# The MLP's first product by Strassen's seven block products, with the tokens stationary

## The chip, the cores and the metric

One Trainium2 chip, one NeuronCore of it. The metric is the device time of one execution in microseconds (us), as a median over runs. The engines named below are TensorE (matmuls, in the profile PE, its weight loads PEld), VectorE (DVE), ScalarE (ACT), GpSimd (POOL) and SyncE (SP, whose queue issues the loads).

## What is computed

A decoder trunk of two layers on 256 tokens of width 2048, all in float32. Each layer has a mixer (differential attention or dilated attention), attention into 256 memory tokens, an output projection, and an MLP with hidden width 8192. The part that matters here:

```
for i in range(DEPTH):                      # 2 layers
    h = _rmsnorm(x, g_attn[i])
    proj = h @ w_in[i]                      # queries, keys, values, memory queries
    ...
    x = x + merged @ w_out[i]
    hm = _rmsnorm(x, g_mlp[i])              # 256 x 2048
    x = x + jnp.square(jax.nn.relu(hm @ w_mlp1[i])) @ w_mlp2[i]   # 2048 x 8192, then 8192 x 2048
return _rmsnorm(x, g_final)
```

## The kernel before

**Precision.** Every large product is made of three. An operand is split into a high part, which TensorE's fp32r format holds, and the low rest; hi x hi, hi x lo and lo x hi are added. `split` does it: ScalarE copies the high part (line 108), VectorE subtracts it for the low part (line 109). Activations are split once; weights are split as they arrive, 1024 columns at a time (`weights`, into the tags whi and wlo with four buffers each), from loads of 1 MB (`load_weights`, tag raw, three buffers, issued by SP, line 72).

**The first product** (`mlp_up`) computes one chunk of 1024 hidden features in four blocks of 256 with `gemm_feat`. The weights are stationary there and the tokens move: for each of 16 row tiles and two halves of the block one matmul takes the high weights against high and low activations side by side (512 columns, line 142) and one the low weights against the high activations (256 columns, line 139). The result has features on the partitions and tokens along the columns. `feat_sum` adds its two halves (lines 214 and 216), VectorE squares its positive part (line 540), and a split writes the two parts of hT.

**The second product** (`mlp_down`) takes hT as the stationary operand and moves split weights of 512 columns (`gemm_tok_piece`, lines 161 to 163): 192 matmuls for a chunk, in four column blocks of 512 whose results go into PSUM tiles psd; two VectorE operations a block (line 562) add them to x.

**Order.** The program emits up(0), up(1), down(0), up(2), down(1), ..., up(7), down(6), down(7) for each layer. A scheduler then fixes the order on each engine before the kernel runs, and assigns buffers from the pools: an instruction whose buffer isn't free is placed where the buffer will be, and waits there on a semaphore. PSUM has two tiles of two banks (pool pmm, tag mm) and four of one bank (pool pat, tag at).

**Names.** ps_u, hi_u, lo_u, raw_u: first product; psd, hi_d, lo_d, raw_d: second product; pso, psv, ps_q, ps_k: output, value, query and key projections; xTm: the activations of the first product; lo_o and lo_d: low halves of weights; x_sb: the tokens.

Of the kernel before, what the change touches and what calls it, by code (L numbers as in the profile page):

```python
# [9 lines left out]
F32 = mybir.dt.float32  # L10
F32R = mybir.dt.float32r
# [6 lines left out]
P = 128  # L18
# [14 lines left out]
TMP = 6  # L33
GROUPS = ((128, 1), (512, 4), (2048, 16))
# [17 lines left out]
def trunk(ctx: ExitStack, tc: tile.TileContext, x, mem, g_attn, w_in, w_out, lambda_qk,  # L52
# [6 lines left out]
    apool = ctx.enter_context(tc.tile_pool(name="apool", bufs=8))  # L59
# [33 lines left out]
    # matmuls on zeros that bring the tensor engine to its full clock while the first loads run  # L93
    zero = const.tile([P, 512], BF16, name="zero")
# [16 lines left out]
    def weights(src, k, c, nm, raw=None):  # L111
        """k row tiles of c columns, k * c = 2048, as two (hi, lo) pairs of k/2 row tiles."""
        if raw is None:
            *_, raw = load_weights(src, k, c, nm)
        res = []
        for h in range(2):
            hi = wpool.tile([P, 1024], F32R, tag="whi", bufs=4, name=f"hi_{nm}_{h}")
            lo = wpool.tile([P, 1024], F32R, tag="wlo", bufs=4, name=f"lo_{nm}_{h}")
            split(hi, lo, raw[:, h * 1024:(h + 1) * 1024])
            for kk in range(k // 2):  # L120
                res.append((hi[:, kk * c:(kk + 1) * c], lo[:, kk * c:(kk + 1) * c]))
        return res

    def gemm_feat(w, acts, nm, raws=(None, None)):
        """[256 features, 256 tokens] as [128, 2, 2, 256]: the two halves of dim 2 add up."""
        ps = pmm.tile([P, 2, 512], F32, tag="mm", name=f"ps_{nm}")
        k0 = 0
        for pc in range(2):
            wt = weights(w[pc * 1024:(pc + 1) * 1024, :], 8, 256, f"{nm}_{pc}", raws[pc])
            for kk in range(8):  # L130
                k = k0 + kk
# [36 lines left out]
    def to_feat(src_of_tok, c, dst, gcol, nm):  # L168
        """tokens x 512 features (chunk c) -> features x tokens times g, split into dst."""
# [14 lines left out]

    def sumsq(src, acc):
# [8 lines left out]
    def rstd_of(ssq, nm):  # L194
        """ssq [128, 2, 4] -> 1 / rms by token [128, 2]."""
# [6 lines left out]
    def bcast_row(r, nm):  # L202
        """[128, 2] by token -> [128, 256], the tokens along the free axis in every partition."""
# [7 lines left out]
    def feat_sum(ps, nm):  # L211
        """the two halves of a gemm_feat result added: [128, 2, 256] in SBUF."""
# [437 lines left out]
```

## Time and profile before

| | us |
|---|---|
| median of 3 runs (2239.68 to 2239.79) | 2239.72 |
| span of the profiled execution | 2237.8 |
| TensorE busy in it | 2226.3 (99%) |
| VectorE busy | 1335.5 (60%) |
| ScalarE busy | 1040.7 (47%) |

The span runs from the first to the last instruction of one profiled execution. The median is 1.9 us above it. Busy time is the time in which an engine had an instruction under way, so neighbours that overlap are counted once there, while the mean duration of a group is that of one instruction by itself. The granted clock tells at which share of its full rate TensorE was allowed to run.

### The profile page before, as it was taken

The page shows a single profiled execution, that of the slowest core. Times are in us where ns is not written, and L with a number is a line of the kernel's source. Part 1 is how long each engine was busy: PE and PEld are TensorE (multiplying, and loading weights), DVE is VectorE, ACT ScalarE, POOL GpSimd, SP SyncE. Part 2 cuts the span into 40 slices and gives each one's busy share as a digit, 9 for nine tenths or more (in the row PEclk, how much of TensorE's full clock was granted, in tenths as well). Part 3 has the DMA queues.
Part 4 walks back from the last instruction along what each step waited for, and adds up shares of the span by engine and source line. Part 5 has one row for each costly group of instructions (what it writes and reads, how often), then busy time and mean ns, then how long its engine had stood idle before and what let it go on. Part 6 is the DMA issues. An engine that isn't in the chain of part 4 may idle for free.

```text
span 2237.8 us, 27970 instructions
## 1 busy us (share of the span) xinstructions
PE 2226.3 (99%) x11462; PEld 1885.6 (84%) x11462; DVE 1335.5 (60%) x1568; ACT 1040.7 (47%) x1362; POOL 14.0 (1%) x26
## 2 busy tenths in 40 slices
PE   9999999999999999999999999999999999999998
PEld 7888878888888888888888888888888888888887
DVE  7557765565555555555666665555656555555555
ACT  7445554544344444444455544454444444434443
POOL 0000000000000000000000000000000000000000
PEclk9999999999999999999999999999999999999999
DMA  8554454566656656666555455456665665665664
GB/s 266 189 178 161 151 169 162 177 187 188 190 188 188 193 186 192 192 189 193 191 187 166 156 170 188 151 188 188 188 189 188 188 188 190 187 195 188 188 203 148
DMA packets 304849, 411.96 MB, mean 184 GB/s; under 512 B 6529, under 2 KB 203346, under 8 KB 304722
## 3 DMA queue, kind: packets, MB, share of 16 engines
q1 hardware_dynamic: 304448, 410.02, 57.7%
q8 instruction: 89, 1.46, 0.3%
q14 instruction: 38, 0.31, 0.0%
q10 hardware_dynamic: 274, 0.17, 0.0%
HBM read 408.07 MB, written 2.10 MB: 183 GB/s over the span
## 4 chain that ended last, share of the span: by engine, by line
PE 98%; DMA 1%; ACT 0%; issue 0%; DVE 0%; SPq 0%; POOL 0%; POOLq 0%; DVEq 0%
PE ps_u L142 21%; PE ps_u L139 11%; PE psd L163 10%; PE psd L162 10%; PE psd L161 10%; PE ps_q L142 4%; PE ps_k L142 4%; PE pso L163 3%; PE pso L161 3%; PE pso L162 3%; PE ps_q L139 2%; PE ps_k L139 2%; PE psv L163 2%; PE psv L162 2%; PE psv L161 2%; PE ps_km L142 1%
## 5 line engine op out<-in xcount | busy, mean ns | idle before, releaser
L142 PE MATMUL ps_u<-xTm,hi_u 128*128 128x512 f32 x2048 | 720.3, 398 | 0.0
L139 PE MATMUL ps_u<-xTm,lo_u 128*128 128x256 f32 x2048 | 564.9, 281 | 0.0
L142 PEld LDWEIGHTS ps_u<-xTm,hi_u 128*128 128x128 f32 x2048 | 381.5, 188 | 89.3
L109 DVE TENSOR_TENSOR lo_u<-raw_u,hi_u 128x1024 fp32r<-128x1024 f32 x256 | 313.1, 1224 | 232.3 <-ACT hi_u L108 230.4
L109 DVE TENSOR_TENSOR lo_d<-raw_d,hi_d 128x1024 fp32r<-128x1024 f32 x252 | 308.3, 1223 | 235.7 <-ACT hi_d L108 233.5
L108 ACT ACTIVATE hi_d<-raw_d 128x1024 fp32r<-128x1024 f32 x252 | 267.3, 1061 | 347.7 <-PE psd L163 293.2
L108 ACT ACTIVATE hi_u<-raw_u 128x1024 fp32r<-128x1024 f32 x256 | 271.1, 1059 | 286.9 <-PE ps_u L142 188.8
L163 PE MATMUL psd<-hi_d,hT 128*128 128x512 f32 x1008 | 392.6, 389 | 0.0
L161 PE MATMUL psd<-hi_d,hT 128*128 128x512 f32 x1008 | 392.4, 389 | 0.0
L162 PE MATMUL psd<-lo_d,hT 128*128 128x512 f32 x1008 | 392.3, 389 | 0.0
L139 PEld LDWEIGHTS ps_u<-xTm,lo_u 128*128 128x128 f32 x2048 | 386.7, 189 | 5.9
L162 PEld LDWEIGHTS psd<-lo_d,hT 128*128 128x128 f32 x1008 | 189.2, 188 | 39.4
L163 PEld LDWEIGHTS psd<-hi_d,hT 128*128 128x128 f32 x1008 | 189.2, 188 | 39.3
L161 PEld LDWEIGHTS psd<-hi_d,hT 128*128 128x128 f32 x1008 | 189.2, 188 | 38.8
L142 PE MATMUL ps_q<-xT,hi_q 128*128 128x512 f32 x384 | 138.0, 399 | 0.0
L142 PE MATMUL ps_k<-xT,hi_k 128*128 128x512 f32 x384 | 136.7, 395 | 0.0
L139 PE MATMUL ps_k<-xT,lo_k 128*128 128x256 f32 x384 | 108.2, 287 | 0.0
L139 PE MATMUL ps_q<-xT,lo_q 128*128 128x256 f32 x384 | 107.9, 286 | 0.0
L562 DVE SCALAR_TENSOR_TENSOR x_sb<-psd,rsq,x_sb 128x512 f32<-128x512 f32 x126 | 88.8, 746 | 24.4 <-PE psd L163 24.4
L214 ACT ACTIVATE fb_u<-ps_u 128x512 f32<-128x512 f32 x64 | 38.3, 598 | 119.0 <-PE ps_u L142 119.0
L216 DVE TENSOR_TENSOR ft_u<-ps_u,fb_u 128x512 f32<-128x512 f32 x64 | 44.3, 692 | 78.8 <-ACT fb_u L214 78.8
L109 DVE TENSOR_TENSOR lo_v<-raw_v,hi_v 128x1024 fp32r<-128x1024 f32 x48 | 58.8, 1225 | 49.7 <-ACT hi_v L108 49.6
(272 smaller groups left out, 2767.2 us busy)
## 6 DMA issues: line engine op xcount, KB each, us to landing
raw_u<-in_w_mlp_dram SPq DMA_DIRECT2D x128, 1024.0 KB, 5.7
raw_d<-in_w_mlp_dram SPq DMA_DIRECT2D x126, 1024.0 KB, 5.1
raw_q<-in_w_in_dram SPq DMA_DIRECT2D x24, 1024.0 KB, 5.2
raw_k<-in_w_in_dram SPq DMA_DIRECT2D x24, 1024.0 KB, 5.1
raw_v<-in_w_in_dram SPq DMA_DIRECT2D x24, 1024.0 KB, 5.0
raw_o<-in_w_out_dram SPq DMA_DIRECT2D x24, 1024.0 KB, 5.1
raw_km<-in_w_mem_kv_dram SPq DMA_DIRECT2D x8, 1024.0 KB, 5.3
raw_vm<-in_w_mem_kv_dram SPq DMA_DIRECT2D x8, 1024.0 KB, 5.0
```

The lines of the kernel that those rows point to most:

```text
L108: nc.scalar.activation(dst_hi, src, AF.Copy)
L109: nc.vector.tensor_tensor(dst_lo, src, dst_hi.bitcast(F32), op=ALU.subtract)
L139: nc.tensor.matmul(ps[:, j, 0:256], lo[:, cols], a[:, 0, :], **f)
L142: nc.tensor.matmul(ps[:, j, :], hi[:, cols], a.rearrange("p h t -> p (h t)"), **f)
L161: nc.tensor.matmul(ps[:, t, :], ah, hi, start=first and kk == 0, stop=False)
L162: nc.tensor.matmul(ps[:, t, :], ah, lo, start=False, stop=False)
L163: nc.tensor.matmul(ps[:, t, :], al, hi, start=False, stop=last and kk == 3)
L214: nc.scalar.activation(b, ps[:, :, 1, :], AF.Copy)
L216: nc.vector.tensor_tensor(t, ps[:, :, 0, :], b, op=ALU.add)
L562: nc.vector.scalar_tensor_tensor(xc[:, t, :], ps[:, t, :], rsq[:, t:t + 1], xc[:, t, :], op0=ALU.mult, op1=ALU.add)
```

## The change

The first product is regrouped. Take two row tiles k, k+1 of the weights and of the activations, the two halves of the tokens (128 each) and two column halves of a chunk (512 each). These are 2 x 2 blocks, and Strassen's scheme gives the four result blocks from seven block products in place of eight. The activations' combinations are made once a layer (`to_comb`, tiles comb): a11, a12, a22, n1 = a22 - a21, m2 = n1 + a11, s4 = m2 - a12, s3 = a11 - a21, each split. The weights' combinations are made by VectorE for each pair of row tiles (`up_weights`): b11, b22, b21 (from o), t1, t3 (from the sum s) and t2, t4, each split. A pair of row tiles is called a step here; a chunk has eight. The tokens' combinations are stationary and the split weights move, 512 columns at a time, so each step has 21 matmuls. They add up over the eight steps in seven PSUM banks: p1 and p2 in p12, p5 and p7 in p57, and p3, p6 and p4. After the last step VectorE makes the four blocks u11, m12, c21, m22 out of the seven, ScalarE applies relu and square, and since the result now has tokens on the partitions, `to_hT` turns it back by 16 transposes a chunk and splits it into hT.

Buffers had to be found for this. The tag up (seven tiles of 128 x 1024) holds the split combinations, ux (five) the raw weights of the first product, ut (two) the sums s. Weight loads elsewhere are 512 KB (three buffers raw), with three pairs of whi and wlo. The memory keys and values of layer 1 are kept in DRAM until they are needed (kv_dram), and the distance tables are built once a layer.

```diff
+KP = KT // 2
+UX = 5
+UT = 2
+UP = 7
+RAW = 3
+WH = 3
...
-    apool = ctx.enter_context(tc.tile_pool(name="apool", bufs=8))
+    apool = ctx.enter_context(tc.tile_pool(name="apool", bufs=11))
+    upool = ctx.enter_context(tc.tile_pool(name="upool", bufs=1))
...
-        raw = wpool.tile([P, 2048], F32, tag="raw", name=f"raw_{nm}")
...
+        raw = wpool.tile([P, 1024], F32, tag="raw", bufs=RAW, name=f"raw_{nm}")
+        nc.sync.dma_start(raw.rearrange("p (k c) -> p k c", c=c), src.rearrange("(k p) c -> p k c", p=P))
...
-            hi = wpool.tile([P, 1024], F32R, tag="whi", bufs=4, name=f"hi_{nm}_{h}")
-            lo = wpool.tile([P, 1024], F32R, tag="wlo", bufs=4, name=f"lo_{nm}_{h}")
...
+        hi = wpool.tile([P, 1024], F32R, tag="whi", bufs=WH, name=f"hi_{nm}")
+        lo = wpool.tile([P, 1024], F32R, tag="wlo", bufs=WH, name=f"lo_{nm}")
...
+    def to_comb(kp, comb, gcol, nm):
+
+        pt = pat.tile([P, 2, 2, P], F32, tag="at", name=f"pc_{nm}")
+        xs = work.tile([P, 2, 2, P], F32, tag="tmp", bufs=TMP, name=f"xs_{nm}")
+        for a in range(2):
+            k = 2 * kp + a
+            for t in range(2):
+                nc.tensor.transpose(pt[:, a, t, :], x_sb[:, t, k * P:(k + 1) * P], ident)
+            nc.scalar.activation(xs[:, a], pt[:, a], AF.Copy, scale=gT[:, gcol + k:gcol + k + 1])
+        cs = work.tile([P, 4, P], F32, tag="tmp", bufs=TMP, name=f"cs_{nm}")
+        a11, a12, a21, a22 = xs[:, 0, 0], xs[:, 1, 0], xs[:, 0, 1], xs[:, 1, 1]
+        n1, m2, s4, s3 = (cs[:, n] for n in range(4))
+        nc.vector.tensor_tensor(n1, a22, a21, op=ALU.subtract)
+        nc.vector.tensor_tensor(m2, n1, a11, op=ALU.add)
+        nc.vector.tensor_tensor(s4, m2, a12, op=ALU.subtract)
+        nc.vector.tensor_tensor(s3, a11, a21, op=ALU.subtract)
+        for n, a in (("p1", a11), ("p2", a12), ("p4", a22), ("p5", n1), ("p6", m2), ("p3", s4), ("p7", s3)):
+            split(comb[n][:, kp, 0, :], comb[n][:, kp, 1, :], a)
+
+    def up_weights(w, kp, f0, nm):
...
+        def pieces(a, k, m):
+            hi = upool.tile([P, k, 512], F32R, tag="up", bufs=UP, name=f"{m}h_{nm}")
+            lo = upool.tile([P, k, 512], F32R, tag="up", bufs=UP, name=f"{m}l_{nm}")
+            split(hi, lo, a)
+            return [(hi[:, n], lo[:, n]) for n in range(k)]
+
+        b = upool.tile([P, 2, 512], F32, tag="ux", bufs=UX, name=f"b_{nm}")
+        nc.sync.dma_start(b, pair(0, 512))
+        o = upool.tile([P, 2, 512], F32, tag="ux", bufs=UX, name=f"o_{nm}")
+        nc.sync.dma_start(o, pair(512, -512))
+        b11, b22 = pieces(b, 2, "b")
+        oh = upool.tile([P, 2, 512], F32R, tag="up", bufs=UP, name=f"oh_{nm}")
+        split(oh[:, 0], oh[:, 1], o[:, 1])
+        s = upool.tile([P, 2, 512], F32, tag="ut", bufs=UT, name=f"s_{nm}")
+        nc.vector.tensor_tensor(s, b, o[:, 0:1].to_broadcast([P, 2, 512]), op=ALU.add)
+        t1, t3 = pieces(s, 2, "s")
+        nc.vector.tensor_tensor(b[:, 0], s[:, 0], b[:, 1], op=ALU.add)
+        nc.vector.tensor_tensor(b[:, 1], b[:, 0], o[:, 1], op=ALU.add)
+        t2, t4 = pieces(b, 2, "t")
+        return {"p1": b11, "p2": (oh[:, 0], oh[:, 1]), "p3": b22, "p5": t1, "p7": t3, "p6": t2, "p4": t4}
...
-        def mlp_up(c):
-            for f in range(4):
-                f0 = c * 1024 + f * 256
-                ps = gemm_feat(w_mlp1[i][:, f0:f0 + 256], xT2, f"u{i}{c}{f}")
...
+        def product(ps, n, kp, hi, lo, last):
+            ah, al = comb[n][:, kp, 0, :], comb[n][:, kp, 1, :]
+            nc.tensor.matmul(ps, ah, hi, start=kp == 0, stop=False)
+            nc.tensor.matmul(ps, ah, lo, start=False, stop=False)
+            nc.tensor.matmul(ps, al, hi, start=False, stop=last)
...
+            for s in range(KP + 2):
+                if s < KP:
+                    wt[s] = up_weights(w_mlp1[i], s, f0, f"{nm}{s}")
+                for lag, names in ((0, ("p1", "p3", "p2")), (1, ("p5", "p7")), (2, ("p6", "p4"))):
+                    if 0 <= s - lag < KP:
+                        for n in names:
+                            product(bank[n], n, s - lag, *wt[s - lag][n], s - lag == KP - 1)
+                if s == KP - 1:
...
+                    nc.scalar.activation(c1, bank["p1"], AF.Copy)
+                    nc.scalar.activation(c3, p3, AF.Copy)
+                    nc.vector.tensor_tensor(c11, c1, bank["p2"], op=ALU.add)
+                    squared(c11, 1.0)
...
+            nc.vector.tensor_tensor(u2, c1, p6, op=ALU.subtract)
+            nc.vector.tensor_tensor(u4, u2, bank["p5"], op=ALU.add)
+            nc.vector.tensor_tensor(u3, u2, bank["p7"], op=ALU.add)
+            nc.vector.tensor_tensor(m22, u3, bank["p5"], op=ALU.add)
+            nc.vector.tensor_tensor(c21, u3, p4, op=ALU.add)
+            nc.vector.tensor_tensor(m12, u4, c3, op=ALU.add)
...
         def mlp_down(c):
             for n in range(4):
+                if c + 1 < NC and n in (1, 2):
+                    to_hT(c + 1, 2 * n - 2)
+                    to_hT(c + 1, 2 * n - 1)
```

The scheduler's order around this, at three places. In the new names the digits are layer, chunk and step; bl, sl and tl are the low halves of b, s and t (all 1024 columns), oh holds both halves of the split o, u11, u21, u12 and u22 are the four result blocks, and pu is the PSUM tile of the transposes back.

VectorE in the first product of layer 0, chunk 3, before: one block of 256 features.

```order
L109 TENSOR_TENSOR lo_u032_0_0_5879<-raw_u032_0_5876,hi_u032_0_0_5878 128x1024
L109 TENSOR_TENSOR lo_u032_0_1_5883<-raw_u032_0_5876,hi_u032_0_1_5882 128x1024
L109 TENSOR_TENSOR lo_u032_1_0_5921<-raw_u032_1_5918,hi_u032_1_0_5920 128x1024
L216 TENSOR_TENSOR ft_u031_5869<-ps_u031_5782,fb_u031_5867 128x512
L540 SCALAR_TENSOR_TENSOR usq031_5871<-ft_u031_5869 128x512
L109 TENSOR_TENSOR lo_u032_1_1_5925<-raw_u032_1_5918,hi_u032_1_1_5924 128x1024
L109 TENSOR_TENSOR hT030_5773<-usq031_5871,hT030_5773 128x2x256
```

VectorE at the same place after: one step, from one split of b to the next.

```order
L112 TENSOR_TENSOR bl_033_6227<-b_033_6222,bh_033_6226 128x1024
L225 TENSOR_TENSOR s_034_6277<-b_034_6266,o_034_6268 128x1024
L112 TENSOR_TENSOR oh_033_6230<-o_033_6224,oh_033_6230 128x512
L227 TENSOR_TENSOR b_033_6222<-s_033_6233,b_033_6222 128x512
L112 TENSOR_TENSOR sl_033_6236<-s_033_6233,sh_033_6235 128x1024
L228 TENSOR_TENSOR b_033_6222<-b_033_6222,o_033_6224 128x512
L112 TENSOR_TENSOR tl_033_6242<-b_033_6222,th_033_6241 128x1024
L112 TENSOR_TENSOR bl_034_6271<-b_034_6266,bh_034_6270 128x1024
```

Four splits for 32 matmul pairs have become seven operations for 21 matmuls, and the same seven stand in each of steps 3 to 7.

TensorE after, at the end of the second product of chunk 1 (psd013) in layer 0: the first product of chunk 3 goes on.

```order
L161 MATMUL psd013_6028<-hi_d01312_6085,hT011_5061 128x512
L600 MATMUL p12_03_6103<-bh_030_6112,cb_p1_0_3428 128x512
L598 MATMUL p12_03_6103<-oh_030_6116,cb_p2_0_3429 128x512
L599 MATMUL p12_03_6103<-oh_030_6116,cb_p2_0_3429 128x512
L600 MATMUL p12_03_6103<-oh_030_6116,cb_p2_0_3429 128x512
L598 MATMUL p12_03_6103<-bh_031_6144,cb_p1_0_3428 128x512
L599 MATMUL p12_03_6103<-bl_031_6145,cb_p1_0_3428 128x512
L600 MATMUL p12_03_6103<-bh_031_6144,cb_p1_0_3428 128x512
```

Up to here 11 matmuls of step 0 have been placed among those of the second product; from here on only first-product matmuls stand until step 7. Before, the second product was one closed run, and so was each block of the first.

VectorE after, behind the first product of chunk 3 (its results t2 to u21), with step 0 of chunk 4 and the weights of the second product (lo_d) between.

```order
L112 TENSOR_TENSOR lo_d02012_6546<-raw_d02012_6543,hi_d02012_6545 128x1024
L228 TENSOR_TENSOR b_040_6821<-b_040_6821,o_040_6823 128x512
L633 TENSOR_TENSOR t2_03_6471<-c1_03_6442,p6_03_6106 128x512
L112 TENSOR_TENSOR lo_d02100_6581<-raw_d02100_6578,hi_d02100_6580 128x1024
L634 TENSOR_TENSOR t4_03_6473<-t2_03_6471,p57_03_6104 128x512
L635 TENSOR_TENSOR t3_03_6472<-t2_03_6471,p57_03_6104 128x512
L112 TENSOR_TENSOR tl_040_6841<-b_040_6821,th_040_6840 128x1024
L112 TENSOR_TENSOR lo_d02102_6599<-raw_d02102_6596,hi_d02102_6598 128x1024
L112 TENSOR_TENSOR hT030_6486<-pu_030_6563,hT030_6486 128x4x128
L636 TENSOR_TENSOR u22_03_6447<-t3_03_6472,p57_03_6104 128x512
L637 TENSOR_TENSOR u21_03_6446<-t3_03_6472,p4_03_6107 128x512
```

The last reader of p57 (u22) has moved behind a split of the next chunk, two weight splits and a split of hT.

## Rows read from the trace of the kernel before

**Rows 1.** The page, part 1: busy time, share, instructions of each engine.

```profile
PE 2226.3 (99%) x11462; PEld 1885.6 (84%) x11462; DVE 1335.5 (60%) x1568; ACT 1040.7 (47%) x1362; POOL 14.0 (1%) x26
```

**Rows 2.** The page, part 4: the chain that ended last, by engine.

```profile
PE 98%; DMA 1%; ACT 0%; issue 0%; DVE 0%; SPq 0%; POOL 0%; POOLq 0%; DVEq 0%
```

**Rows 3.** That chain in order of time (start us, us, what), one chunk.

```profile
606.75 0.45 PE ps_u L142 x2
...
618.05 0.45 PE ps_u L142 x2
...
629.35 0.45 PE ps_u L142 x2
...
695.49 0.45 PE ps_u L142 x2
```

**Rows 4.** Busy time by stretch: kernel start, a first product, a second product.

```profile
core 0: us, PE busy (x) PEld busy (x) DVE busy (x) ACT busy (x) POOL busy (x), PEclk, DMA share, GB/s
...
0.00:5.00 5.00, 3.81 (x9) 1.34 (x10) 3.40 (x10) 1.28 (x1) 3.12 (x13) 1.00 0.53 140
...
606.75:651.95 45.20, 45.20 (x243) 38.77 (x243) 27.33 (x29) 21.58 (x25) 0.00 (x0) 1.00 0.60 189
651.95:695.49 43.54, 43.54 (x208) 36.52 (x207) 24.74 (x24) 16.84 (x16) 0.00 (x0) 1.00 0.63 191
```

**Rows 5.** Waits, longest in total: who waited for whom, us, times, longest.

```profile
ACT hi_d L108 <- PE psd L163: 293.2, 177, 1.9
DVE lo_d L109 <- ACT hi_d L108: 233.5, 160, 1.9
DVE lo_u L109 <- ACT hi_u L108: 230.4, 154, 1.6
```

**Rows 6.** Groups by line and shape: busy us, mean ns of one, idle before.

```profile
L142 PE MATMUL ps_u<-xTm,hi_u 128*128 128x512 f32 x2048 | 720.3, 398 | 0.0
...
L163 PE MATMUL psd<-hi_d,hT 128*128 128x512 f32 x1008 | 392.6, 389 | 0.0
...
L109 DVE TENSOR_TENSOR lo_u<-raw_u,hi_u 128x1024 fp32r<-128x1024 f32 x256 | 313.1, 1224 | 232.3 <-ACT hi_u L108 230.4
...
L562 DVE SCALAR_TENSOR_TENSOR x_sb<-psd,rsq,x_sb 128x512 f32<-128x512 f32 x126 | 88.8, 746 | 24.4 <-PE psd L163 24.4
...
L216 DVE TENSOR_TENSOR ft_u<-ps_u,fb_u 128x512 f32<-128x512 f32 x64 | 44.3, 692 | 78.8 <-ACT fb_u L214 78.8
```

**Rows 7.** TensorE's timeline (start, us): the opening matmuls, six transposes in a row.

```profile
1.19 5.97 PE L98 MATMUL pw<-zero 128*128 128x512 bf16 x14 [1.19 <-DVE zero L95]
...
414.15 0.27 PE L175 MATMUL pt_xm<-ident,x_sb 128*128 128x128 f32 x1
...
414.49 0.82 PE L175 MATMUL pt_xm<-ident,x_sb 128*128 128x128 f32 x6
```

**Rows 8.** VectorE's timeline: operations back to back, and after a wait.

```profile
418.58 2.39 DVE L109 TENSOR_TENSOR lo_o<-raw_o,hi_o 128x1024 fp32r<-128x1024 f32 x2
...
423.81 1.65 DVE L182 SCALAR_TENSOR_TENSOR xTm<-pt_xm,gT,xTm 128x256 fp32r<-128x256 f32 x4
...
642.27 0.69 DVE L540 SCALAR_TENSOR_TENSOR usq<-ft_u 128x512 f32<-128x512 f32 x1
642.88 1.22 DVE L109 TENSOR_TENSOR lo_d<-raw_d,hi_d 128x1024 fp32r<-128x1024 f32 x1
...
650.24 1.23 DVE L109 TENSOR_TENSOR lo_d<-raw_d,hi_d 128x1024 fp32r<-128x1024 f32 x1 [1.48 <-ACT hi_d L108]
651.82 1.41 DVE L562 SCALAR_TENSOR_TENSOR x_sb<-psd,rsq,x_sb 128x512 f32<-128x512 f32 x2 [0.35 <-PE psd L163]
```

**Rows 9.** ScalarE's timeline at two of those waits.

```profile
643.00 0.63 ACT L108 ACTIVATE hT<-usq 128x512 fp32r<-128x512 f32 x1 [0.54 <-DVE usq L540]
...
649.14 1.06 ACT L108 ACTIVATE hi_d<-raw_d 128x1024 fp32r<-128x1024 f32 x1 [1.65 <-PE psd L163]
```

**Rows 10.** Loads and stores: KB each, median us from issue to landing.

```profile
raw_d<-in_w_mlp_dram SPq DMA_DIRECT2D x126, 1024.0 KB, 5.1
...
x_sb<-in_x_dram SPq DMA_DIRECT2D x4, 512.0 KB, 6.9
...
out_dram<-ot SPq DMA_DIRECT2D x8, 256.0 KB, 2.4
```

More of the change, by code (lines that the diff above doesn't have):

```diff
@@ L83, in trunk @@
         nc.sync.dma_start(x_sb[:, :, sl], x[0].rearrange("(t p) d -> p t d", p=P)[:, :, sl])
-        next(first[c // 2])
-    first_raw = [next(f) for f in first]
+        first_raw.append(load_weights(w_in[0][sl, 3 * MIXW:3 * MIXW + 256], 4, 256, f"qm00_{c}"))
     ident = const.tile([P, P], F32, name="ident")
@@ L113, in weights, with gemm_feat @@
         if raw is None:
[L114 to L131 removed]
+            raw = load_weights(src, k, c, nm)
+        hi = wpool.tile([P, 1024], F32R, tag="whi", bufs=WH, name=f"hi_{nm}")
+        lo = wpool.tile([P, 1024], F32R, tag="wlo", bufs=WH, name=f"lo_{nm}")
+        split(hi, lo, raw)
+        return [(hi[:, kk * c:(kk + 1) * c], lo[:, kk * c:(kk + 1) * c]) for kk in range(k)]
+    def gemm_feat(w, acts, nm, raws=(None,) * 4):
+        ps = pmm.tile([P, 2, 512], F32, tag="mm", name=f"ps_{nm}")
+        for pc in range(4):
+            wt = weights(w[pc * 512:(pc + 1) * 512, :], 4, 256, f"{nm}_{pc}", raws[pc])
+            for kk in range(4):
+                k = 4 * pc + kk
                 hi, lo = wt[kk]
@@ L328, in mem_head @@
         for q in range(2):
-            nc.tensor.matmul(sc[:, q, :], qT[:, q * P:(q + 1) * P], kmT[:, i, h, :], start=True, stop=True)
+            nc.tensor.matmul(sc[:, q, :], qT[:, q * P:(q + 1) * P], km_of(i, h), start=True, stop=True)
         nmax = small.tile([P, 2], F32, tag="nmax", name=f"nmax_{nm}")
@@ L517, in trunk @@
                 nc.vector.tensor_tensor(xc[:, t, :], xc[:, t, :], ps[:, t, :], op=ALU.add)
-            xt = act_tile(f"xTm{i}_{c}")
-            to_feat(lambda t: x_sb[:, t, :], c, xt, (2 + i) * KT, f"xm{i}{c}")
-            xT2.append(xt)
+            for kp in (2 * c, 2 * c + 1):
+                to_comb(kp, comb, (2 + i) * KT, f"xm{i}{kp}")
             for t in range(2):
@@ L543, in trunk, with to_hT @@
+        def to_hT(c, n):
+            u, t, f = ublk[c][n]
+            pt = pat.tile([P, 4, P], F32, tag="at", name=f"pu_{i}{c}{n}")
+            for k in range(4):
+                nc.tensor.transpose(pt[:, k], u[:, k * P:(k + 1) * P], ident)
+            cols = slice(t * P, (t + 1) * P)
+            split(hT[c, f][:, :, 0, cols], hT[c, f][:, :, 1, cols], pt)
         final = i == DEPTH - 1
@@ L576, in trunk @@
         mlp_up(0)
+        for n in range(4):
+            to_hT(0, n)
         for c in range(NC):
@@ L589, in trunk @@
         r0 = DFF - 1024 + f * 512
-        wt.append(weights(w_mlp2[DEPTH - 1][r0:r0 + 512, n0:], 4, 512, f"last{f}"))
+        for h in range(2):
+            wt += weights(w_mlp2[DEPTH - 1][r0 + h * 256:r0 + (h + 1) * 256, n0:], 2, 512, f"last{f}{h}")
     def add_last(t, c0, c1, acc):
```

148 lines of the change are left out of this document (88 added, 60 removed).

## The prediction

> **What bounds the kernel now.** I read the page from the top down. TensorE is busy for 99% of the span [rows 1], and the chain of work that ended last is 98% TensorE [rows 2], so any time has to come out of its stream. The MLP alternates between two phases. One chunk of 1024 hidden features takes 88.74 us, from the first-product matmul at 606.75 to the one at 695.49 [rows 3]: four blocks of 11.30 us (45.20 us) for the first product, then 43.54 us for the second product of the chunk before. TensorE is busy for all of both stretches at a granted clock of 1.00, VectorE for 27.33 and 24.74 us [rows 4]. ScalarE and VectorE have room: their commonest wait is for TensorE to release a split buffer, and next VectorE's for ScalarE's high half [rows 5]. A matmul's listed duration (398 or 389 ns, [rows 6]) overlaps its neighbours and is no price. The price is the distance between starts: 43.54 us / 192 = 0.227 us for 512 moving columns, 45.20 us / 128 = 0.353 us for a pair of 512 and 256 columns.
>
> **TensorE's share of the change.** A chunk's first product had 128 such pairs, 45.20 us. Now it has 7 products x 8 pairs of row tiles x 3 = 168 matmuls of 512 columns, in the form of the second product (activations stationary, split weights moving): 168 x 0.227 = 38.1 us. Added are 16 transposes; six in a row took 0.82 us of which the last alone is 0.27 [rows 7], so 0.11 us each, 1.8 us. TensorE saves 5.3 us a chunk; over 16 chunks 85 us, giving 2155 us if nothing else came to bind.
>
> **VectorE's step.** Each of the eight steps of a chunk (two row tiles of weights) has four VectorE operations on 1024 columns (splits of b, s and t, and the sum s) and three on 512 (split of o, two sums). Such splits run at 1224 ns, alone, 692 ns for 512 [rows 6]. Back to back a 1024 follows another after 2.39 - 1.22 = 1.17 us and a 512 after 1.41 - 0.75 = 0.66 us [rows 6, 8]; so 4 x 1.17 + 3 x 0.66 = 6.7 us. The Trainium skill ("VectorE: DVE Perf Modes", Terms, DRAIN) says that the pipe empties before the next operation can issue; whole durations would make the step 4 x 1.224 + 3 x 0.692 = 7.0 us, some 30 us more over the kernel. By that rule a start would never come before the end ahead of it; the trace has such starts [rows 8], so the sum goes by them.
>
> To this comes a wait. The VectorE excerpt of the order shows that the second sum into b (line 228) stands directly ahead of the split tl of that same b, and the high half th lies between them on ScalarE. Nothing else is queued in the gap. The sum takes 0.69, ScalarE starts 0.04 later, takes 1.06, and VectorE starts 0.04 after that [rows 8, 9]: 1.83 us in place of 0.66. The step becomes 7.8 us. TensorE needs 21 x 0.227 = 4.8 us of it. A second cycle is nearly as long: the load of o for step n+2 takes the slot that the second sum of step n gives up, and sum s(n+2) stands behind it; from the start of s to the end of that second sum are 1.17 + 0.66 + 0.66 + 1.17 + 0.69 = 4.35 us, and a 512 KB load lies between 2.4 us (256 KB, a store) and 5.1 us (1 MB) [rows 10], by interpolation 3.3, an estimate: 7.65 us. I take 7.9. The bounds are 6.7 (no wait) and 8.5 (a load of 4.1).
>
> **Why it does not spread.** Averaged over a chunk VectorE would fit: 8 x 6.7 + 11 x 0.66 (seven sums of results, four low halves of hT) + 16 x 1.17 + 8 x 0.66 (second product) = 85 us. But one step fills all seven slots of "up", and the five of "ux" hold two and a half steps of raw weights, so in the second product's 43.5 us VectorE can prepare little more than step 0 and half of step 1. The order agrees: behind the last matmul of one second product, TensorE's stream holds the rest of steps 0 and 1 and steps 2 to 7 without any other work between.
>
> **One chunk, in sequence.** Count from the end of the second product. Its last eviction and one split take VectorE to 2.9 us. TensorE does 13 waiting products (2.9 us), then those of p5 and p7 of step 0, whose bank the eviction releases (4.3 us); only then is a slot free for th of step 1: ScalarE to 5.4, VectorE's tl to 6.6, s of step 3 and step 2 with its wait to 14.5. Steps 3 to 6 at 7.9: 46.1. In step 7 u11, which releases the bank of p1 and p2, ends 6.2 us in: 52.3 us. Then the next second product starts. On TensorE it is 43.5 us, the first-product matmuls that stand within it (17 to 23, taken as 23) 5.2, transposes 1.8. It also meets a wait: its second block needs the bank of p5 and p7, whose last reader m22 (u22 in the order) stands on VectorE behind the split tl of step 0, two weight splits and hT, and ends some 14.8 us after u11, where TensorE arrives after 12.5: 2.3 us. Together 52.8. The chunk is 105 us against 88.7, so +16.4, six times per layer: +98.
>
> Chunks 0 and 1 have no second product between them, so VectorE sets both: behind the output projection 1.4 + 1.2 + 6.7 (step 1) + 5.7 (22 pieces of to_comb at 0.26: a 256-wide piece takes (1.65 - 0.48) / 3 = 0.39 [rows 8], less 128 / 512 of the 0.51 between 1024 and 512) + 6 x 7.9 = 62; then 7.3 for the results and 8 x 7.9 less 1.6: 69. 131 against 90.4: +41. The second product of chunk 6 has six up matmuls, the transposes and the wait: +5. A layer: 98 + 41 + 5 = 144; two layers: **+288 us**.
>
> **Outside the first product.** to_comb has 22 small VectorE operations for two row tiles where to_feat had four of 256 columns per two tiles: 5.7 against 1.6 us, in a phase where VectorE has as many weight splits as in the second product, so hidden but for late weight splits. Weight buffers are 512 KB instead of 1 MB and three split pairs instead of four: 3 x 2.72 us of matmuls lie in them, and a slot turns round in 0.4 + 3.3 + 1.06 + 1.22 = 6 us, so a burst on VectorE of more than 2 us can now reach TensorE. Such bursts are 36 heads' softmax and 16 to_comb; at 0 to 1.2 us each 0 to 60; I take 20 (0.4 each). The extra copy of kv to DRAM and back, the distance tables and the issue of twice as many loads on SP lie beside other work: 0. Without that cover a 1 MB copy would cost its 5.1 us once each way.
>
> **Sum.** 2237.8 (span) + 288 + 20 = 2545.8; the median is 1.9 above the span: 2548, say 2550 us. Of the 128 steps some 100 lie on this path, 36 in chunks 2 to 7 and 14 in chunks 0 and 1 of each layer. Lower bound of this case: steps of 6.9 (-100), no bank wait (14 x 2.3 = -32), nothing outside (-20): 2400. Upper: steps of 8.5 (+60), outside 60 (+40): 2650.
>
> **Rivals.**
> 1. *TensorE's clock drops in the first product.* There TensorE works 4.8 of 7.9 us, in pieces with gaps between. At the lower level a 512-column matmul takes 5.97 / 14 = 0.427 us (the 14 matmuls that open the kernel, [rows 7], run at that rate, 512 columns at 1.2 GHz, though the window there lists 1.00 [rows 4]); the step would be 21 x 0.427 = 9.0 us, or up to 9.6 with a wait at its seams, +1.1 to 1.7 in some 100 steps: 2660 to 2720. Against it: every stretch read shows 1.00 [rows 4], but none has such gaps. The Trainium skill ("TensorE: Matmul & The Clock Gate", A second HAM failure mode: psum-queue depth-cycling) tells of a kernel whose frequent short idles made the clock swing between its two rates; by that rule this would happen here. No row of this trace can test it. Chance 0.11.
> 2. *VectorE is spread after all, and the kernel gets faster.* If it ran ahead through the second product, the chunk would cost the larger of TensorE's 38.1 + 1.8 + 43.5 = 83.4 and VectorE's 85 us: -3.7 x 16 = -60, 2180 to 2200 with the outside. It decides where the part of the first product that nothing covers falls from 52 us below 36. For: 25 of 43.5 us are all that VectorE does now in the second product [rows 4]. Against: the seven slots. Chance 0.05, with 0.02 more for landing within 0.2% of before.
> 3. *The halved weight buffers bind everywhere.* If a 512 KB load lands only after 6.9 us, as in the opening of the kernel with several in flight [rows 10], a slot turns in 9.6 us against 8.2: +0.47 us for each of some 510 pieces, 240 us: 2790. Against: the opening moves more than the 190 GB/s of the MLP. Chance 0.06.
> 4. *The change does not do what it says* (fewer matmuls): excluded by the order, 2688 matmuls of 512 columns for 2048 + 2048.
>
> **Chances.** The forecast, a first product set by VectorE, 0.76. The range 2430 to 2690 takes in most of it and the near end of rival 1. A measurement here can tell about 0.2%, 4 us: faster 0.05, same 0.02, slower 0.93.
>
> **What the next profile should show.** TensorE's busy share near 85% with idle before the matmuls of lines 598 to 600 released by VectorE and ScalarE; VectorE busy near 76%; starts of successive bl splits in steps 3 to 7 some 7.8 us apart with a gap of 1.2 us before tl released by th; chunk to chunk 105 us; granted clock 1.00. Chunks under 89 us, a gap before s released by a DMA, or a granted clock under 1 would each refute a step.

## The result: 2525.9 us, and the profile after

The changed kernel takes 2525.9 us (median of 4, 2520.5 to 2528.3) where the kernel before takes 2239.7: 1.127 times as long, 95% interval 1.126 to 1.129. The profiled execution has a span of 2523.2 us, 285.4 more than before.

The first row is part 1 of the page of the changed kernel, to be set beside [rows 1]; the other two are its part 4, the chain of work that ended last, by engine and by line, beside [rows 2].

```profile
PE 2284.1 (91%) x10310; PEld 1774.2 (70%) x10310; DVE 1852.8 (73%) x2338; ACT 1286.2 (51%) x1826; POOL 18.4 (1%) x34
...
PE 60%; DVE 16%; DMA 13%; issue 8%; ACT 3%; SPq 0%; POOL 0%; DVEq 0%; POOLq 0%; ACTq 0%
DMA o<-in_w_mlp_dram 12%; PE psd L159 8%; PE psd L161 7%; PE psd L160 7%; PE ps_k L140 4%; PE ps_q L140 4%; DVE b L228 3%; DVE oh L112 3%; DVE b L227 3%; PE p L598 2%; DVE sl L112 2%; PE p L599 2%; PE p L600 2%; PE ps_q L137 2%; PE ps_k L137 2%
```

There are 1152 fewer TensorE instructions, but the chain, 98% TensorE before, is now 60%: VectorE and the load of o have entered it. One steady step of the first product shows how. The rows are VectorE's timeline (start, us, line, operation; in brackets the idle time before it and what ended it), then SP's, which issues the loads.

```profile
786.54 1.22 DVE L112 TENSOR_TENSOR bl<-b,bh 128x1024 fp32r<-128x1024 f32 x1
788.07 1.23 DVE L225 TENSOR_TENSOR s<-b,o 128x1024 f32<-128x1024 f32 x1 [0.32 <-DMA o<-in_w_mlp_dram]
789.22 0.68 DVE L112 TENSOR_TENSOR oh<-o,oh 128x512 fp32r<-128x512 f32 x1
789.82 0.69 DVE L227 TENSOR_TENSOR b<-s,b 128x512 f32<-128x512 f32 x1
790.42 1.22 DVE L112 TENSOR_TENSOR sl<-s,sh 128x1024 fp32r<-128x1024 f32 x1
791.55 0.69 DVE L228 TENSOR_TENSOR b<-b,o 128x512 f32<-128x512 f32 x1
793.42 1.23 DVE L112 TENSOR_TENSOR tl<-b,th 128x1024 fp32r<-128x1024 f32 x1 [1.19 <-ACT th L111]
794.57 1.22 DVE L112 TENSOR_TENSOR bl<-b,bh 128x1024 fp32r<-128x1024 f32 x1
796.08 1.23 DVE L225 TENSOR_TENSOR s<-b,o 128x1024 f32<-128x1024 f32 x1 [0.29 <-DMA o<-in_w_mlp_dram]
```

```profile
784.27 0.37 SPq L220 DMA_DIRECT2D o<-in_w_mlp_dram  x1
...
792.30 0.37 SPq L220 DMA_DIRECT2D o<-in_w_mlp_dram  x1
```

From bl to bl are 8.03 us: two waits, 1.19 and about 0.3, and 6.5 us of operations back to back. The wait before tl is the one that the order showed: the second sum (line 228) stands directly ahead, and ScalarE writes th in between. The wait before s closes a second cycle: s starts at 788.07, the second sum ends at 792.24 and frees the slot, the load of o is issued at 792.30, and 3.78 us later the next s starts: 4.17 + 0.06 + 3.78 = 8.01.

This second cycle is the one that sets the step. It has no slack, and the wait for th is no part of it: tl stands behind the second sum. VectorE's own round, with the wait for th but without the one for the load, is 6.5 + 1.19 = 7.7 us, and the 0.3 us before s is what VectorE then still waits for the load. The chain that ended last says the same. These are its longest pieces in one step of chunk 2 (start, us, what); they go from load to load, by way of s (not among the longest), oh and the second sum, and no tl is among them.

```profile
679.39 3.69 DMA o<-in_w_mlp_dram
683.67 0.64 issue
684.31 0.69 DVE oh L112
685.67 0.98 issue
686.65 0.70 DVE b L228
687.40 3.81 DMA o<-in_w_mlp_dram
```

The groups show that these two waits are the rule (busy us, mean ns of one | idle before, what ended most of it); the third row, for the wait for a bank, is the second product's first matmul of each three (hi x hi). The 30.9 us before s come in 82 of the 128 steps.

```profile
L112 DVE TENSOR_TENSOR tl<-b,th 128x1024 fp32r<-128x1024 f32 x128 | 156.7, 1224 | 103.7 <-ACT th L111 103.6
...
L225 DVE TENSOR_TENSOR s<-b,o 128x1024 f32<-128x1024 f32 x128 | 156.7, 1224 | 31.3 <-DMA o<-in_w_mlp_dram 30.9
...
L159 PE MATMUL psd<-hi_d,hT 128*128 128x512 f32 x1008 | 397.2, 394 | 22.9 <-DVE u L636 22.6
```

One chunk lies between the last evictions of two second products (VectorE's timeline); u of line 630 is the first result block (u11 in the order).

```profile
766.11 1.41 DVE L677 SCALAR_TENSOR_TENSOR x_sb<-psd,rsq,x_sb 128x512 f32<-128x512 f32 x2 [0.40 <-PE psd L161]
...
777.45 1.22 DVE L112 TENSOR_TENSOR tl<-b,th 128x1024 fp32r<-128x1024 f32 x1 [1.18 <-ACT th L111]
...
816.16 0.68 DVE L630 TENSOR_TENSOR u<-c,p 128x512 f32<-128x512 f32 x1
...
870.06 1.41 DVE L677 SCALAR_TENSOR_TENSOR x_sb<-psd,rsq,x_sb 128x512 f32<-128x512 f32 x2 [0.86 <-PE psd L161]
```

870.06 - 766.11 = 103.95 us for a chunk that took 88.74 [rows 3]: 50.7 to the end of u11, then 53.2 for the second product with what stands in it. The six such intervals of layer 0 sum to 616.3 us against 532.4 before (+83.9). From the last eviction of the output projection to the end of the first second product are 180.4 against 134.5 us (+45.9). So the MLP of layer 0 costs 129.8 us more. By the same marks that of layer 1 costs 126.1 (45.8 and 80.3). The other 29.5 of the 285.4 us lie outside: 19.5 up to the end of layer 0's output projection, 6.5 in layer 1's attention and 3.6 at the end of the kernel.

### The profile page after: what moved, and what is told of

It reads as the page before. It is cut to its first block, busy times and chain, and to the rows that moved or that the text cites. A ratio compares the mean times of both kernels' runs of the same rounds, so it can differ in the third digit from the quotient of the medians.

```text
span 2523.2 us, 28147 instructions
## 1 busy us (share of the span) xinstructions
PE 2284.1 (91%) x10310; PEld 1774.2 (70%) x10310; DVE 1852.8 (73%) x2338; ACT 1286.2 (51%) x1826; POOL 18.4 (1%) x34
## 4 chain that ended last, share of the span: by engine, by line
PE 60%; DVE 16%; DMA 13%; issue 8%; ACT 3%; SPq 0%; POOL 0%; DVEq 0%; POOLq 0%; ACTq 0%
DMA o<-in_w_mlp_dram 12%; PE psd L159 8%; PE psd L161 7%; PE psd L160 7%; PE ps_k L140 4%; PE ps_q L140 4%; DVE b L228 3%; DVE oh L112 3%; DVE b L227 3%; PE p L598 2%; DVE sl L112 2%; PE p L599 2%; PE p L600 2%; PE ps_q L137 2%; PE ps_k L137 2%
## 5 line engine op out<-in xcount | busy, mean ns | idle before, releaser
L159 PE MATMUL psd<-hi_d,hT 128*128 128x512 f32 x1008 | 397.2, 394 | 22.9 <-DVE u L636 22.6
L111 ACT ACTIVATE th<-b 128x1024 fp32r<-128x1024 f32 x128 | 135.4, 1058 | 385.1 <-DVE b L228 365.2
L112 DVE TENSOR_TENSOR tl<-b,th 128x1024 fp32r<-128x1024 f32 x128 | 156.7, 1224 | 103.7 <-ACT th L111 103.6
L599 PE MATMUL p<-sl,cb_p 128*128 128x512 f32 x256 | 112.8, 441 | 79.1 <-DVE sl L112 79.1
L225 DVE TENSOR_TENSOR s<-b,o 128x1024 f32<-128x1024 f32 x128 | 156.7, 1224 | 31.3 <-DMA o<-in_w_mlp_dram 30.9
L112 DVE TENSOR_TENSOR bl<-b,bh 128x1024 fp32r<-128x1024 f32 x128 | 156.1, 1220 | 19.8 <-PE p L600 12.3
L112 DVE TENSOR_TENSOR sl<-s,sh 128x1024 fp32r<-128x1024 f32 x128 | 156.1, 1220 | 0.2 <-ACT sh L111 0.2
L111 ACT ACTIVATE sh<-s 128x1024 fp32r<-128x1024 f32 x128 | 134.1, 1048 | 15.1 <-PE p L599 14.1
L111 ACT ACTIVATE bh<-b 128x1024 fp32r<-128x1024 f32 x128 | 133.7, 1044 | 6.5 <-DMA b<-in_w_mlp_dram 4.7
L598 PE MATMUL p<-sh,cb_p 128*128 128x512 f32 x256 | 103.6, 405 | 10.0 <-DVE u L636 8.2
L598 PE MATMUL p<-bh,cb_p 128*128 128x512 f32 x256 | 98.0, 445 | 15.5 <-ACT bh L111 15.5
```

What stands on the lines that cost most here:

```text
L111: nc.scalar.activation(dst_hi, src, AF.Copy)
L112: nc.vector.tensor_tensor(dst_lo, src, dst_hi.bitcast(F32), op=ALU.subtract)
L159: nc.tensor.matmul(ps[:, t, :], ah, hi, start=first and kk == 0, stop=False)
L225: nc.vector.tensor_tensor(s, b, o[:, 0:1].to_broadcast([P, 2, 512]), op=ALU.add)
L598: nc.tensor.matmul(ps, ah, hi, start=kp == 0, stop=False)
L599: nc.tensor.matmul(ps, ah, lo, start=False, stop=False)
```

## The experiments

The theory was the prediction's: VectorE's order, with the wait for th and the cycle through the load of o, sets the step. The rivals were TensorE with its clock, and the loads as such. A time with an interval is a median of four executions (nine in the last run) beside the kernel before; a time without one is a single execution. Leaving out sums, or sharing one operand tile, gives other values than the reference; of those runs only the time is read.

### Less work on VectorE, more on TensorE

**Leaving out the two t sums:**

```diff
-        nc.vector.tensor_tensor(b[:, 0], s[:, 0], b[:, 1], op=ALU.add)
-        nc.vector.tensor_tensor(b[:, 1], b[:, 0], o[:, 1], op=ALU.add)
```

> The two t sums are left out: th and tl are split from b as it was loaded, so p4 and p6 are products with other data. VectorE has five operations a step instead of seven. Theory (VectorE sets the step): the step falls by the two sums (1.33) and by the wait for th that hangs on the second (1.19), to 5.2 back to back, up to 5.6: some 100 steps by 2.4 to 2.8 us, 240 to 280 us less: 2245 to 2285. Rival 1 (TensorE at a reduced clock sets it): at half rate a step would be 9, at full rate 4.8; the time would stay within 50 us of 2526. Rival 2 (loads set it): step 7.5 or more, 2470 to 2505.

Measured: 2249.7 us, 276 less than the changed kernel, at the upper end of 240 to 280. Steady steps are 5.15 us from bl to bl.

**Leaving out all three sums** (the sum s too; the splits of s and t take b):

> The changed kernel without the three sums s and t: the splits of s and t take b as it was loaded, so four of the seven products have other data. VectorE has 3 x 1.17 + 0.66 = 4.2 us a step, TensorE 4.8. Theory: with VectorE below it TensorE sets the whole MLP, a chunk is 38.1 + 1.8 + 43.5 = 83.4 us to 88, and the time 2155 plus what lies outside (20 to 60): 2170 to 2250 us; this is what the 24 matmuls fewer per chunk pair are worth when nothing else binds. Rival (loads: 1 MB per 4.8 us is more than the 190 GB/s of the MLP before): VectorE and TensorE wait for DMA in the first product, step 6 or more, 2280 or more.

Measured: 2186.0 us. Its page, parts 1 and 4, and its chunk:

```profile
PE 2157.3 (99%) x10310; PEld 1789.4 (82%) x10310; DVE 1554.7 (71%) x1954; ACT 1301.4 (60%) x1826; POOL 17.5 (1%) x34
...
PE 95%; DVE 2%; issue 1%; ACT 1%; DMA 0%; POOL 0%; SPq 0%; POOLq 0%; DVEq 0%; ACTq 0%
```

```profile
687.91 1.41 DVE L673 SCALAR_TENSOR_TENSOR x_sb<-psd,rsq,x_sb 128x512 f32<-128x512 f32 x2 [0.40 <-PE psd L161]
...
771.85 1.41 DVE L673 SCALAR_TENSOR_TENSOR x_sb<-psd,rsq,x_sb 128x512 f32<-128x512 f32 x2 [0.40 <-PE psd L161]
```

With the same matmuls and loads, TensorE is busy for 99% and a chunk takes 83.94 us; the prediction's 38.1 + 1.8 + 43.5 made 83.4. So the saving on TensorE is real: without the sums the kernel is 54 us faster than the one before. What takes it away is the sums on VectorE: from 2186.0 to 2525.9 they and the waits that hang on them cost 340 us. The rate of the loads is excluded as the limit: the same number per step landed in time for steps of 4.76 us. The time of a single load is another matter, since the cycle holds one.

**More matmuls:** every product of steps 1 to 6 repeats one.

```diff
             nc.tensor.matmul(ps, al, hi, start=False, stop=last)
+            if not last and 0 < kp:
+                nc.tensor.matmul(ps, al, hi, start=False, stop=False)
```

> Steps 1 to 6 of every chunk repeat the third matmul of each of their seven products (42 more 512-column matmuls a chunk, 672 in all, 152 us of TensorE at 0.227 us each); the sums of the products are thereby other numbers. Theory (VectorE sets the step): TensorE's 4.8 us a step become 6.4, still under 8.0, so the steady step does not change; only the matmuls of step 1, done behind the second product where TensorE is the later one, cost: 0 to 1.6 us a chunk, 0 to 25 us: 2526 to 2551. If TensorE set the time, 152 us more: 2678. Rival (the clock): with TensorE busy for 6.4 of 8 us instead of 4.8 the granted clock in the first product stays at 1.00 instead of dipping to 0.81 to 0.9 in some windows; if the dips cost time now, the kernel gets faster in spite of the extra matmuls, 2490 to 2520.

Measured: 2527.2 us, 1.3 more. The rows are the same 10 us of a first product in the changed kernel and in this one (length, busy time of PE, PEld, DVE, ACT and POOL, granted clock, DMA share, GB/s).

```profile
790.00:800.00 10.00, 7.91 (x24) 5.03 (x25) 8.53 (x10) 3.47 (x4) 0.00 (x0) 0.83 0.35 105
```

```profile
790.00:800.00 10.00, 9.02 (x37) 6.46 (x37) 7.99 (x9) 4.62 (x6) 0.00 (x0) 1.00 0.49 142
```

672 more matmuls, 152 us of them, cost nothing that can be told: TensorE was waiting anyway. And the clock, which in the changed kernel falls to its lower level (1.2 GHz) for part of some windows, stays at the upper (2.4 GHz) here (mean 0.990 against 0.983) without a gain. Strictly, a gain from the clock could have been offset by the extra matmuls, up to the 25 us allowed for them. The steps themselves speak against it: in the changed kernel the two from 786.54 to 802.57, over the stretch at 0.83, take 8.03 and 8.00 us, the one before, at 1.00, 7.95 (bl to bl).

### Moving the waits

**The t sums written into o instead of b:**

```diff
-        nc.vector.tensor_tensor(b[:, 0], s[:, 0], b[:, 1], op=ALU.add)
-        nc.vector.tensor_tensor(b[:, 1], b[:, 0], o[:, 1], op=ALU.add)
-        t2, t4 = pieces(b, 2, "t")
+        nc.vector.tensor_tensor(o[:, 0], s[:, 0], b[:, 1], op=ALU.add)
+        nc.vector.tensor_tensor(o[:, 1], o[:, 0], o[:, 1], op=ALU.add)
+        t2, t4 = pieces(o, 2, "t")
```

> The two t sums are written into o instead of b: the same number of instructions of each kind, the same result. The raw slot of b comes free after the first t sum, and in VectorE's order the sum s of the step after next now stands between the second t sum and the split tl, so that it runs while ScalarE writes th. Theory (VectorE's order and the two waits in it set the step): both waits go (1.19 us before tl, 0.30 before s), the steady step falls from 8.02 to its back-to-back 6.54, at most 6.9; with some 100 steps on the path that is 110 to 150 us: 2375 to 2415 us. Rival 1 (the clock, or another limit on TensorE, sets the step): TensorE's matmuls stay as they are, the step stays at 7.8 to 8.0: 2500 to 2526. Rival 2 (the weight loads set the step, two of 512 KB per step): the wait before tl only moves to a wait of s for its load, step 7.5 to 7.8: 2470 to 2505.

Measured: 2671.2 us (ratio to before 1.193, interval 1.191 to 1.195), a clear miss. The group of s, a step of VectorE, and SP:

```profile
L225 DVE TENSOR_TENSOR s<-b,o 128x1024 f32<-128x1024 f32 x128 | 156.7, 1224 | 225.1 <-DMA o<-in_w_mlp_dram 223.0
```

```profile
829.40 1.22 DVE L112 TENSOR_TENSOR bl<-b,bh 128x1024 fp32r<-128x1024 f32 x1
...
835.62 1.23 DVE L225 TENSOR_TENSOR s<-b,o 128x1024 f32<-128x1024 f32 x1 [2.67 <-DMA o<-in_w_mlp_dram]
836.76 1.22 DVE L112 TENSOR_TENSOR tl<-o,th 128x1024 fp32r<-128x1024 f32 x1
...
838.50 1.22 DVE L112 TENSOR_TENSOR bl<-b,bh 128x1024 fp32r<-128x1024 f32 x1
```

```profile
830.64 0.37 SPq L220 DMA_DIRECT2D o<-in_w_mlp_dram  x1
```

The wait before tl is gone: s runs in it. But that s belongs two steps ahead, and its load of o now takes the slot that bl gives up: issued at 830.64, just behind bl, needed after only oh, sl and the second sum, landed after 4.8 us. The step is 838.50 - 829.40 = 9.10 us. The expectation had counted two waits that both go; but the cycle through the load already set the step, and the edit made it longer, from 8.0 to 9.1 us. The order had shown s ahead of tl; I had not asked in which slot its load lands, nor behind which operation. (The granted clock is 0.943 here, with TensorE busy for 88% of the span; the chain of this run too goes from load to load, in steps of 9 us.)

**One buffer for s instead of two**, the sums in b as in the changed kernel (the three distance tables, which used the same buffers, get their own):

```diff
-        s = upool.tile([P, 2, 512], F32, tag="ut", bufs=UT, name=f"s_{nm}")
+        s = upool.tile([P, 2, 512], F32, tag="us", bufs=1, name=f"s_{nm}")
```

> The changed kernel with one buffer for the sum s instead of two (the three distance tables get buffers of their own); same work, same result. With a second s buffer the program put s of a step far ahead; with one it stands between the second t sum and the split tl of the step before, so that VectorE has 1.17 us of work while ScalarE writes th. Theory (the wait for th and the cycle through the load of o set the step together): the wait before tl (1.19) goes; the load of o now takes the slot of b that tl gives up, and from there to its sum s lie about 4.2 us of VectorE, against 0.4 + 3.7 to 4.8 us for the load: a wait of 0 to 1 us before s stays. Step 6.6 to 7.6 instead of 8.02, some 100 steps: 2385 to 2485 us. Rival (the clock or another limit on TensorE): no change, 2510 to 2530.

Measured: 2383.3 us (ratio to before 1.064, interval 1.062 to 1.065), 143 us under the changed kernel. A steady step on VectorE, and the group of tl:

```profile
744.35 1.22 DVE L112 TENSOR_TENSOR bl<-b,bh 128x1024 fp32r<-128x1024 f32 x1
745.48 0.68 DVE L112 TENSOR_TENSOR oh<-o,oh 128x512 fp32r<-128x512 f32 x1
746.08 0.69 DVE L227 TENSOR_TENSOR b<-s,b 128x512 f32<-128x512 f32 x1
746.68 1.22 DVE L112 TENSOR_TENSOR sl<-s,sh 128x1024 fp32r<-128x1024 f32 x1
747.82 0.69 DVE L228 TENSOR_TENSOR b<-b,o 128x512 f32<-128x512 f32 x1
748.42 1.22 DVE L225 TENSOR_TENSOR s<-b,o 128x1024 f32<-128x1024 f32 x1
749.69 1.23 DVE L112 TENSOR_TENSOR tl<-b,th 128x1024 fp32r<-128x1024 f32 x1
750.83 1.22 DVE L112 TENSOR_TENSOR bl<-b,bh 128x1024 fp32r<-128x1024 f32 x1
```

```profile
L112 DVE TENSOR_TENSOR tl<-b,th 128x1024 fp32r<-128x1024 f32 x128 | 156.7, 1225 | 5.6 <-ACT th L111 1.5
```

The seven operations stand back to back, 6.48 us a step in place of 8.0; both waits are gone. In layer 0 a chunk takes 43 to 45 us up to the end of u11, where the changed kernel takes some 51, and some 51 for the rest in place of 52 to 54. Fewer buffers made it faster, because the one buffer keeps s from being put far ahead: it now stands between the second sum and tl. What is left, 2383 against 2186 without sums, goes with a step of 6.48 us in place of 4.76. Of the runs with the changed first product that compute the reference this is the fastest, and it is still 6% slower than the kernel before.

**One s buffer and the t sums in o:**

> As the run with one s buffer, and the two t sums are written into o instead of b; same result. The run with t in o and two s buffers was slower because s of the step after next stood before tl of this one, and its load started only with the bl before it: 2.4 us of VectorE lay over a load of 4.8. Here s of the next step stands there, and about 8 us of VectorE lie between the split that frees the slot and the sum that needs the load. Theory (VectorE's order and its two waits set the step): both waits go, step 6.54 to 6.8, some 100 steps by 1.2 to 1.5 us: 2375 to 2405 us. Rival (two 512 KB loads per step cannot land faster than some 9 us, whatever the order): about 2670, as with two s buffers. Rival (clock): 2500 or more.

Measured: 2411.9 us (ratio 1.077, interval 1.075 to 1.078): 7 us above the range. The steady step is 6.49 us as well, so the loads follow any order that gives them time. Its chunk is longer (99.3 against some 95 us). Some 1 to 2 us of that come before the end of u11: less of step 1 stands inside the second product (of its splits only bl, where the kernel above has bl, oh and both sums). Some 3 us come behind it; TensorE's wait for u22 is 27.3 us in all against 16.8, and the rest of them was not traced.

### Room to spread

On top of the kernel just described, one operand tile stands for all seven; the space goes to splits and raw weights of odd steps (14 slots instead of 7, 9 instead of 5).

```diff
...
-        comb = {n: act_comb(f"{n}_{i}") for n in PRODUCTS}
+        one = act_comb(f"p1_{i}")
+        comb = {n: one for n in PRODUCTS}
...
```

> As the run before it, and all seven products read and write one operand tile instead of seven (so their values are others; number and size of all operations stay). The freed space holds the splits and raw weights of odd steps: 14 slots for splits instead of 7, 9 for raw weights instead of 5. Theory (the first product does not spread because one step fills the split slots): VectorE's order now has 1 to 2 steps more ahead of the end of the second product, so 6.6 to 9 us of each of 12 to 14 chunks go under TensorE's second product: 80 to 120 us less than the run before it, 2265 to 2320 if that one is at 2385. Rival (the second product's own splits and the results leave VectorE no room there): within 30 us of the run before it.

Measured: 2335.1 us, 77 less than the kernel it builds on, just under the 80 to 120 expected. The six intervals of layer 0 average 91.6 us against 97.4, 5.9 less. That is a difference of two changes: to the end of u11 a chunk takes 33 to 36 us against 44 to 46, some 11 less or more than one and a half steps, while the rest takes 55 to 60 against 53.7. So more slots do move VectorE's work under the second product, as the theory said, and the second product pays back part of it. It needs space that the kernel does not have.

### The sums on GpSimd

```diff
-        nc.vector.tensor_tensor(s, b, o[:, 0:1].to_broadcast([P, 2, 512]), op=ALU.add)
+        nc.gpsimd.tensor_tensor(s, b, o[:, 0:1].to_broadcast([P, 2, 512]), op=ALU.add)
```

and the two t sums likewise, into o; the three sums also stand earlier in the program.

> As the run with t in o, and all three sums of a step (s, 1024 columns, and the two t sums, 512 each) run on GpSimd, which is idle there. Same result. Theory: VectorE's step is then 3 x 1.17 + 0.66 = 4.2 us, below the 4.8 of TensorE, so the step is set by TensorE, or by GpSimd if its three sums take longer. No row shows GpSimd on such a tile. If it does them in VectorE's time (2.5 us a step) the chunk becomes some 85 to 92 us and the kernel 2200 to 2300, near or below the kernel before. The point of decision is 4.8 us for the three; at three times VectorE's time (7.5 us) the step is 7.5 to 8 and the time 2480 to 2530, no gain over the changed kernel. Rival (TensorE's clock sets it): 2500 or more whatever GpSimd takes.

Measured: 2661.2 us (ratio 1.188, interval 1.186 to 1.190), worse than the bad end of the range. GpSimd's and VectorE's timelines of the same 6 us:

```profile
703.58 2.76 POOL L223 TENSOR_TENSOR s<-b,o 128x1024 f32<-128x1024 f32 x1 [1.84 <-DMA o<-in_w_mlp_dram]
706.42 2.15 POOL L226 TENSOR_TENSOR o<-s,b 128x512 f32<-128x512 f32 x1
```

```profile
704.01 3.41 DVE L112 TENSOR_TENSOR bl<-b,bh 128x1024 fp32r<-128x1024 f32 x1
707.34 1.77 DVE L112 TENSOR_TENSOR oh<-o,oh 128x512 fp32r<-128x512 f32 x1
```

GpSimd needs 2.7 + 2.1 + 2.1 = 6.9 us for the three sums. On top, bl takes 3.41 instead of 1.22 us: it ends 1.08 us after GpSimd's s (706.34), and oh 0.54 after the next sum (708.57). It looks as if VectorE does its work only when GpSimd's instruction is over. The Trainium skill ("SBUF — State Buffer", SBUF: two separate sides) says so: a VectorE operation with two SBUF inputs and GpSimd share a pair of ports, and whoever comes second waits for the whole instruction. The trace agrees, with these numbers. So VectorE is busy for longer (1896.7 against 1852.8 us) with 384 operations fewer, and the expectation, which put VectorE's step at 4.2 us as if it were alone, was wrong in that term.

This does not make the meeting of the two engines the cause of the 135 us over the changed kernel. The nearest run is the one with the t sums in o and two s buffers, 2671.2 us with a step of 9.10; here two steps (bl at 696.55 and at 714.74) take 18.19, and the time is 10 us less. GpSimd's s waits for its load of o as VectorE's did there, 379.3 us in all. What the meeting costs by itself no run separates.

### The weight buffers by themselves

The kernel before with raw tiles of 512 KB (three) and three pairs of split tiles:

> The kernel before with the weight buffers of the change and nothing else of it: raw tiles of 512 KB, three of them, and three pairs of split tiles instead of four; the memory tokens and the output tiles get two buffers of their own. Same result. Theory (a slot turns round in 6 us, three pairs hold 8.2 us of matmuls, and only the 36 bursts of softmax on VectorE can reach TensorE): 0 to 40 us more, 2240 to 2280. Rival (rival 3 of the prediction: several 512 KB loads in flight land so late that 0.47 us is lost for each of some 510 pieces): 2480. The part of the change outside the first product was put at 20 us, this and the many small operations of to_comb together.

Measured: 2245.6 us (ratio 1.0027, interval 1.0017 to 1.0037): 6 us. Rival 3, which put 240 us on them, falls.

## Why the prediction was right, step by step

The median, 2525.9, lies 24 under the 2550 forecast and inside the range. The mechanism was the forecast one in the main: VectorE's order, with two waits in it, sets the step of the first product, and TensorE waits. Of the two cycles that the prediction weighed, though, the other one binds, and two terms of the sum missed by amounts that, by luck, partly cancel (the MLP and what lies outside it, below).

- **TensorE's share.** 83.4 us a chunk predicted; 83.94 measured where VectorE no longer binds.
- **VectorE's step.** 6.7 back to back predicted, 6.5 measured; with the wait for th 7.8 predicted, and 1.19 us of wait is what stands there (1.17 by the sum: 1.83 less 0.66). The sum from starts was right. The one from whole durations (7.0), by the rule on DRAIN in the Trainium skill ("VectorE: DVE Perf Modes", Terms), was not: bl starts at 744.35 for 1.22 and oh at 745.48. The cycle through the load was put at 4.35 + 3.3 = 7.65; it is 4.17 + 0.06 + 3.78. The load, estimated from stores of 256 KB and loads of 1 MB, was too short by 0.5, the VectorE part too long by 0.2.
- **Which cycle binds.** The prediction had the wait for th set the step (7.8) and the load come second (7.65), and it named a gap before s released by a DMA as a sign against it. That gap is there, 0.3 us in 82 steps: the load's cycle, 8.0, sets the step, and the one with th would be 7.7. Taken 7.9, above both sums, measured 8.0: that the step came out so close is in part luck.
- **The chunk in sequence.** To the end of step 2's tl 14.5 predicted, 12.6 measured (778.67 - 766.11); to the end of u11 52.3 against 50.7; the rest 52.8 against 53.2; the chunk 105 against 103.95. The overestimate is the opening, where tl of step 1 was put at 6.6 us and ends at 4.8. The bank's wait was there, released by u22 (line 636): 22.6 us in 12 times, 1.9 each, for 14 times 2.3.
- **Sum of the MLP.** 144 us a layer predicted, 130 and 126 measured. Of the 14 us in layer 0 some 4 lie in chunks 0 and 1 with the first second product, some 10 in the six intervals, the openings above all. Over both layers 288 predicted, 256 measured: this is the most mis-sized term.
- **Outside.** 20 predicted, 29.5 measured, which hides part of the miss in the MLP. The small buffers by themselves are 6 of it. The prediction laid the rest to to_comb and softmax. The trace shows another part that it did not have: step 0 and the s of step 1 of chunk 0 are placed into the attention of layer 0. There that s waits 3.74 us for its load of o, VectorE's work for the attention stands behind it, and TensorE waits 6.07 us for that work (up to 391.42). Without the three sums layer 0's output projection ends 13 us earlier (467.56 against 480.67 for its last eviction). What remains was not traced.
- **Why it does not spread.** One step's worth of slots: with a second one the stretch up to u11 became some 11 us shorter, 6 of which remained in the chunk.
- **Not as predicted: the clock.** I had written 1.00 and that less would refute a step. It is 0.983 in the mean, 0.83 in windows of the first product, so rival 1's mechanism does occur. Its price was wrong: the step does not become 9 us, since TensorE does not set it and the dips are short. TensorE's busy share is 91% where 85% was predicted, VectorE's 73% where 76% was; a matmul is listed longer here than before (443 ns in the mean for those of th; 398 for those of ps_u [rows 6]), and what else makes up the differences was not traced.

## What to carry to other kernels

An algorithm that saves matmuls by sums of operands moves work to the engine that makes the operands; with 256 tokens to each weight, seven splits and sums for every 21 matmuls were too many here, and the price is set per step, where nothing else covers it, not by average busy shares. Before such a change, write the producing engine's step in its order with its waits, follow each buffer round (who frees it, which load takes it, who needs that load), and compare the longest of these cycles with the consumer's step. A wait that shows in the timeline need not be the one that sets the step; the chain tells which is. A deeper buffer is no gain in itself: here it let the order put work ahead of what it waits for.

## What the runs showed of the hardware that was not expected

- A GpSimd sum of 128x1024 takes 2.4 to 2.8 us and of 128x512 2.1 us, against 1.22 and 0.69 on VectorE, and a VectorE operation on two SBUF tiles that meets it ends 1.08 (1024 columns) or 0.54 us (512) after it.
- A 512 KB load lands in 3.7 us in the median where the last one was issued some 5.6 us ahead of it (o in the changed kernel), in 4.2 some 2.4 us behind another (b there), and in 4.8 some 1.7 us behind another (o in the kernel with t in o).
- In the first product, where TensorE's matmuls come in pieces with waits between them, the granted clock was 0.83 over one stretch of 10 us; with the matmuls repeated it was 1.00 over the same stretch. No cost of it could be told.
